# Block 2's short-lived attention buffers in a pool of their own, with residual rows and routing table loaded into its room, and the overflow branch behind the final combine

## The chip, the cores and the metric

The kernel runs on one core of one Trainium2 chip. The metric is the time on the device of one execution, in microseconds (us), as the median of several runs. The engines are named as in the profile: PE multiplies matrices (PEld loads its weights), DVE, ACT and POOL work on rows, SP issues DMA transfers, and ACT and POOL issue some too. The span of a profiled execution runs from its first to its last instruction; the execution's own time is a little longer.

## The reference: two transformer blocks

The input is 512 tokens of 1024 values in fp32. Block 1 is a sparse attention with a state space mixer and a mixture of 16 experts; the change touches it in nothing but a name. Block 2, in outline:

```python
h = rms_norm(x, norm_attn)
q_mla, ckv, k_rope, qkv_dil, gate_pre = split(h @ w_in)
om = mla_branch(q_mla, ckv, k_rope, ...)       # 8 heads, causal softmax attention
od = dilated_branch(qkv_dil, ...)              # 3 groups (dilation 1, 4, 16), merged by their log sums
m  = gate0 * (om @ w_o_mla) + gate1 * (od @ w_o_dil)
x  = x + m @ w_out
hf = rms_norm(x, norm_ffn)
combine = top 2 of the 8 experts of the best of 4 groups, with weights   # T x 32
for e in range(32):
    y += combine[:, e:e+1] * ((silu(hf @ w_gate[e]) * (hf @ w_up[e])) @ w_down[e])
out = x + y
```

## The kernel before: stages, pools and the places that the change touches

The 512 tokens are NT = 4 tiles of 128 rows (P). Products in fp32 are made of three products of split halves: `whi`, `wlo` for weights, `ahi`/`alo`-like names (`hhi`, `mhi`, `mlo`, `odh`, `odl`, `omh`, `oml`) for rows. ACT copies the high half, DVE or POOL subtract it for the low one. A scheduler that follows the program with times of its own sets the order of the instructions on each engine; waits follow from buffers and data. Buffers come from pools, stacked on the left and the right side of the on-chip memory. A pool's room can be taken by the next one only when all that used it are done.

Block 2 runs `block2`, from the main function: projections, MLA attention (`mla_att`), three dilated groups (`dil_att`), whose results go to DRAM (`accd`), and gates. The **merge** follows. `merge_groups` (L1555 on) reads the small tables `nmd`, forms the factors `mcf` (ACT, L1569), and for each tile loads three `da` (SP, L1583), multiplies them by the factors (DVE, L1585) and adds them up in `od` (POOL, L1587). PE turns `od` over (into a bank `tp`, L266), ACT and DVE split it into `odh` and `odl` (L173, L174). `split_mla` does the same for the MLA output `omT` (L1601, L1602). `merge_out` multiplies both by the halves of `wo`, applies the gates (`ga`, `gb`), and splits the sum into `mhi`, `mlo`. Then the product with `wo2` is added to the **residual rows** `xo` (DVE, L1897), four tiles that SP loads from DRAM (`xr`, L1866). The router's weight table `wr` is loaded by ACT (L768, in `moe_open`) and multiplied by the norm's gains `cl` on POOL (L1876). Both live in pool `rt2`, which is opened when block 2's pool `b2` is closed.

The **second mixture** is `moe_experts_rows`, for 32 experts with 64 places each. The weights of each expert are streamed (SP, L823: `raw` and `rawp`, from `in_wgu` and `in_wd`). PE gathers the tokens of four experts by a one-hot matrix (`sel`, L1164), multiplies by gate and up (`gu`, L1179), and by down (`down`, L1208). The weighted result `yy` (ACT for odd, DVE for even experts; L1218, L1220) has two buffers, and POOL scatters it with an adding indirect DMA into `xa` in DRAM (L1221). `xa` holds the rows that the experts' results are added to. The last LAST = 2 experts stay on the chip: `tokens` and `combined` add them with matmuls. SP loads the four tiles of `xa` back (`spare<-xa`, L1227) when all scatters are in.

The **end**: `moe_overflow` reads a count (L1263) and branches around its body when it is zero (L1264); the body handles tokens that found no place in their expert. Every engine has its own copy of the branch. Behind it, the main function combines: 32 matmuls (L1257), two banks `sc` and `pv` in turn, eight adds (L1924), four stores by ACT and SP in turn (L1925).

## Time and profile before

| | us |
|---|---|
| median of 3 runs | 1420.57 |
| lowest and highest of them | 1415.96, 1423.95 |
| the profiled execution, its own time | 1421.81 |
| its span | 1420.0 |

| engine | busy, us | share of the span |
|---|---|---|
| PE | 1313.9 | 93% |
| PEld | 1006.4 | 71% |
| DVE | 776.3 | 55% |
| ACT | 591.3 | 42% |
| POOL | 453.1 | 32% |

Shares over the whole span mix stages with different limits. The merge lies at about 980 to 1108 us of the span, the second mixture's experts at 1118 to 1400, and the end behind them. A row of the timeline gives start, duration, engine, line, operation, and in brackets the idle time just before it with what ended it. A row of waits gives what was waited for, the total in us, the times, and the longest. "L1221" is line 1221 of the kernel before.

### The profile page before, as it was taken

How to read it: one execution, taken by the hardware profiler on the slowest of the kernel's cores; microseconds unless marked ns; L12 is line 12 of the kernel's file. 1: busy time of each engine (PE TensorE's matmuls, PEld its weight loads, DVE VectorE, ACT ScalarE, POOL GpSimd, SP SyncE). 2: the span in 40 equal slices, each digit the busy share in tenths (PEclk: the TensorE clock that was granted, in tenths of full speed). 3: DMA queues.
4: the chain of work that ended last, by engine and by line, in shares of the span. 5: the costliest groups of instructions: out<-in, count | busy, mean ns of one | idle time of the engine just before them, and what ended most of it. 6: DMA issues, size and time to landing. Idle time of an engine off the chain costs nothing. (4 is left out here: it accounts for less than half of the span.)

```text
span 1420.0 us, 21542 instructions
## 1 busy us (share of the span) xinstructions
PE 1313.9 (93%) x8172; PEld 1006.4 (71%) x8188; DVE 776.3 (55%) x1659; ACT 591.3 (42%) x1235; POOL 453.1 (32%) x368
## 2 busy tenths in 40 slices
PE   8898999779999798999999999999989699998976
PEld 8786778756665597977899999887779545444423
DVE  7899964858785756665454353226543623222222
ACT  5466442336665355564654453444323222211211
POOL 3354642422221246531142242215532201111111
PEclk9999999879999899999999999999999899999997
DMA  6122114889997212210111222234249589999993
GB/s 235 60 75 75 45 41 173 303 292 299 315 295 272 96 46 83 90 53 38 60 69 68 76 77 96 69 108 162 89 171 328 191 305 358 365 356 365 368 365 130
DMA packets 68980, 250.77 MB, mean 177 GB/s; under 512 B 12354, under 2 KB 12610, under 8 KB 62720
## 3 DMA queue, kind: packets, MB, share of 16 engines
q1 hardware_dynamic: 56304, 220.90, 43.2%
q0 software_dynamic: 11408, 25.24, 6.6%
q10 hardware_dynamic: 1152, 3.12, 0.6%
q8 instruction: 68, 1.11, 0.3%
q14 instruction: 48, 0.39, 0.1%
HBM read 230.29 MB, written 26.71 MB: 181 GB/s over the span
## 5 line engine op out<-in xcount | busy, mean ns | idle before, releaser
L154 POOL TENSOR_TENSOR wlo<-raw,whi 128x1024 fp32r<-128x1024 f32 (+4 forms) x62 | 149.4, 2412 | 250.3 <-ACT whi L153 250.3
L153 ACT ACTIVATE whi<-raw 128x1024 fp32r<-128x1024 f32 (+4 forms) x172 | 178.3, 1038 | 95.8 <-PE mm L183 41.9
L154 DVE TENSOR_TENSOR wlo<-raw,whi 128x1024 fp32r<-128x1024 f32 (+3 forms) x110 | 142.6, 1296 | 100.7 <-ACT whi L153 100.3
L1221 POOL DMA_INDIRECT xa<-yy,idx x30 | 46.6, 1553 | 223.0 <-DMA xa<-yy,idx 146.1
L183 PE MATMUL mm<-whi,hRl 128*128 128x256 f32 x384 | 109.5, 286 | 0.0
L181 PE MATMUL mm<-whi,hhi 128*128 128x256 f32 (+2 forms) x352 | 103.7, 294 | 5.0 <-ACT qraw L1412 1.9
L1179 PE MATMUL mm<-raw,xe 128*64 128x512 f32 x396 | 101.3, 620 | 4.5 <-ACT xe L1168 4.5
L183 PE MATMUL mm<-whi,hlo 128*128 128x256 f32 (+2 forms) x352 | 102.8, 292 | 0.0
L181 PE MATMUL mm<-whi,hRh 128*128 128x256 f32 x352 | 102.6, 291 | 0.0
L182 PE MATMUL mm<-wlo,hhi 128*128 128x256 f32 (+2 forms) x352 | 102.1, 290 | 0.0
L182 PE MATMUL mm<-wlo,hRh 128*128 128x256 f32 x352 | 99.8, 283 | 0.0
L271 POOL TENSOR_TENSOR hss<-hss,mh 128x4 f32<-128x4 f32 (+1 forms) x64 | 60.0, 939 | 103.8 <-DVE hss L270 92.6
L181 PEld LDWEIGHTS mm<-whi,hhi 128*128 128x128 f32 x352 | 69.4, 197 | 10.7 <-issue 3.8
L1186 DVE TENSOR_TENSOR gul<-gul,mm 64x512 f32<-64x512 f32 x32 | 21.9, 685 | 100.1 <-ACT gul L1185 99.9
L183 PEld LDWEIGHTS mm<-whi,hRl 128*128 128x128 f32 x384 | 74.0, 193 | 0.0
L1164 PEld LDWEIGHTS pv<-sel,xh 128*128 128x128 f32 x256 | 49.6, 194 | 29.9 <-issue 25.8
L182 PEld LDWEIGHTS mm<-wlo,hhi 128*128 128x128 f32 x352 | 69.5, 197 | 1.6 <-issue 1.4
L183 PEld LDWEIGHTS mm<-whi,hlo 128*128 128x128 f32 x352 | 69.5, 197 | 1.4 <-issue 1.1
L1164 PE MATMUL pv<-sel,xh 128*128 128x256 f32 x256 | 67.3, 298 | 2.1 <-issue 2.1
L181 PEld LDWEIGHTS mm<-whi,hRh 128*128 128x128 f32 x352 | 67.2, 191 | 0.2
L182 PEld LDWEIGHTS mm<-wlo,hRh 128*128 128x128 f32 x352 | 67.3, 191 | 0.0
L1179 PEld LDWEIGHTS mm<-raw,xe 128*64 128x64 f32 x396 | 28.2, 141 | 53.2 <-issue 43.4
(533 smaller groups left out, 3685.4 us busy)
## 6 DMA issues: line engine op xcount, KB each, us to landing
raw<-in_wgu SPq DMA_DIRECT2D x163, 512.0 KB, 6.2
raw<-in_wd SPq DMA_DIRECT2D x77, 512.0 KB, 6.3
raw<-in_w2b SPq DMA_DIRECT2D x26, 1024.0 KB, 4.9
rawp<-in_wgu SPq DMA_DIRECT2D x29, 512.0 KB, 5.6
raw<-in_wo SPq DMA_DIRECT2D x12, 1024.0 KB, 4.8
rawp<-in_wd SPq DMA_DIRECT2D x19, 512.0 KB, 5.8
raw<-in_w1b SPq DMA_DIRECT2D x8, 1024.0 KB, 4.9
spare<-xa SPq DMA_DIRECT2D x8, 512.0 KB, 4.9
```

Of the source, the lines that this page charges most:

```text
L153: self.nc.scalar.activation(hi[:, :n], src, AF.Copy)
L154: eng.tensor_tensor(lo[:, :n], src, hi[:, :n].bitcast(F32), op=OP.subtract)
L181: nc.tensor.matmul(ps, lh, rh, start=start and i == 0, stop=False)
L182: nc.tensor.matmul(ps, lh, rl, start=False, stop=False)
L183: nc.tensor.matmul(ps, ll, rh, start=False, stop=stop and i == n - 1)
L271: return self.nc.gpsimd.tensor_tensor(out, out, self.mh[:, :n], op=OP.pow)
L1164: nc.tensor.matmul(pg[:, j * 256:(j + 1) * 256], part[t][:, c], sels[e][:, t].rearrange("p e s -> p (e s)"), start=(i == 0), stop=(i == le ...
L1179: nc.tensor.matmul(pg[j * T:(j + 1) * T], x[:, 2 * c + j, e % 4], w[:, j * 512:(j + 1) * 512], start=(c == 0), stop=(c == 3))
L1186: V.tensor_tensor(lo, lo, pg[o * T:(o + 1) * T], op=OP.add)
L1221: nc.gpsimd.indirect_dma_start(out=xa2, out_offset=bass.IndirectOffsetOnAxis(ap=self.idx[:, 0, e:e + 1], axis=0), in_=y, in_offset=None, b ...
```

## The change

1. Block 2's short-lived tiles (the probabilities `pr` and their turned copies `pe`, the MLA output `omT`, the dilated groups' `ab` and `row`) come from a pool `bs` of their own on the right side ("b2s") and not from `b2`. In block 1 the name stands for the old pool.
2. `block2` takes a function and calls it ahead of `merge_out`. It closes that pool, opens `rt2` in its room, and there issues the loads of the four `xo`, and `moe_open` with the load of `wr`. The pool of the weights, `mw2`, is opened after `b2` is closed, as before.
3. The experts' results get three buffers (NY = 3) of twice the width, of which one half is used, in place of two.
4. The final combine stands in `moe_experts_rows`, ahead of `moe_overflow`. It uses the banks `sc`, `pv`, `mm` and `tp`, and the last tile is stored in two halves, by SP and ACT. In the overflow body, each tile is stored again.

```diff
-        pr = self.b1.tile([P, 512], F32, tag="pr", name="pr", bufs=self.NPR)
+        pr = self.bs.tile([P, 512], F32, tag="pr", name="pr", bufs=self.NPR)
...
-        omT = self.omT = b1.tile([P, 4, S], F32, name="omT")
+        omT = self.omT = self.bs.tile([P, 4, S], F32, name="omT")
...
-            y = me.tile([P, 512], F32, tag="yy", name="yy", bufs=2)
+            y = me.tile([P, D], F32, tag="y", name="yy", bufs=self.NY)[:, :512]
...
+        for t in range(NT):
+            x = self.base[t]
+            for n in range(2):
+                c = slice(n * 512, (n + 1) * 512)
+                o = bank(("sc", "pv", "mm", "tp")[2 * (t % 2) + n])
+                self.combined(o, t, n)
+                V.tensor_tensor(x[:, c], x[:, c], o, op=OP.add)
+                if t == NT - 1:
+                    (nc.sync, nc.scalar)[n].dma_start(self.A["out"][t * P:(t + 1) * P, c], x[:, c])
+            if t < NT - 1:
+                self.store(t, x)
         self.moe_overflow(me)
+
+    def store(self, t, x):
+        (self.nc.sync if t % 2 else self.nc.scalar).dma_start(self.A["out"][t * P:(t + 1) * P, :], x)
...
                 if rows is None:
                     nc.sync.dma_start(self.xa[t * P:(t + 1) * P, :], acc)
+                else:
+                    self.store(t, acc)
...
-    def block2(self):
+    def block2(self, then):
+
...
+        then()
         self.merge_out()
...
         with self.pool("b1") as self.b1:
+            self.bs = self.b1
             self.block1()
...
+        nmw, nme = 19, 1
+        self.LAST = 2
+        self.NX, self.NY, self.FLIGHT = 0, 3, 4
+        self.FIRST = 3
+        xs, xl, short = [], [], ExitStack()
+
+        def experts2():
+
+            short.close()
+            rt = mws.enter_context(right("rt2"))
+            for t in range(NT):
+                xs.append(rt.tile([P, D], F32, tag=f"xo{t}", name=f"xo{t}"))
+                nc.sync.dma_start(xs[t], self.xr[t * P:(t + 1) * P, :])
+            xh = rt.tile([P, NT, D], F32R, name="xh")
+            self.moe_open(32, 64, A["wr2"], self.r("br2"), A["wgu2"], A["wd2"], rt, None, 0, ([xh[:, t] for t in range(NT)], xl))
         with self.pool("b2") as self.b1:
+            self.bs = short.enter_context(right("b2s"))
             self.dmat = self.b1.tile([P, 512], BF, name="dmat")
             dm = self.g("dm")
             nc.scalar.dma_start(dm, A["dm"])
             nc.vector.tensor_copy(self.dmat, dm)
-            self.block2()
-        rt = mws.enter_context(right("rt2"))
-        xs = [rt.tile([P, D], F32, tag=f"xo{t}", name=f"xo{t}") for t in range(NT)]
-        xl = []
-        for t in range(NT):
-            nc.sync.dma_start(xs[t], self.xr[t * P:(t + 1) * P, :])
-        nmw, nme = 19, 1
-        self.LAST = 2
-        self.NX, self.NY, self.FLIGHT = 0, 2, 4
-        self.FIRST = 3
+            self.block2(experts2)
+        rt, xh = self.rt, self.rows[0]
+        self.mw = mws.enter_context(right("mw2"))
+        self.places = [(self.mw, f"raw{i}") for i in range(nmw)]
         xp = ph.enter_context(self.pool("x2"))
-        xh = rt.tile([P, NT, D], F32R, name="xh")
         self.pp = xp
-        self.moe_open(32, 64, A["wr2"], self.r("br2"), A["wgu2"], A["wd2"], rt, mws.enter_context(right("mw2")), nmw,
-                      ([xh[:, t] for t in range(NT)], xl))
...
         self.moe_mid(ph, None, "2", nme)
-        for t in range(NT):
-            x = self.base[t]
-            for n in range(2):
-                c = slice(n * 512, (n + 1) * 512)
-                o = self.bank(("sc", "pv")[n])
-                self.combined(o, t, n)
-                nc.vector.tensor_tensor(x[:, c], x[:, c], o, op=OP.add)
-            (nc.sync if t % 2 else nc.scalar).dma_start(A["out"][t * P:(t + 1) * P, :], x)
         mws.close()
```

What this does to the order of instructions is shown at three places. SP's queue at the merge, first before, then after:

```order
L1583 DMA da<-accd_73 128x512
L146 DMA raw<-in_wo 128x2048
L1583 DMA da<-accd_71 128x512
...
L146 DMA raw<-in_wo 128x2048 x5
L1866 DMA xo_11273<-xr 128x1024
...
L146 DMA raw<-in_wo 128x2048
L823 DMA raw<-in_wgu 128x1024 x12
```

```order
L1599 DMA da<-accd_73 128x512
L1887 DMA xo_10970<-xr 128x1024
...
L146 DMA raw<-in_wo 128x2048
L1599 DMA da<-accd_71 128x512
...
L146 DMA raw<-in_wo 128x2048 x5
L823 DMA raw<-in_wgu 128x1024 x2
L146 DMA raw<-in_wo 128x2048
L823 DMA raw<-in_wgu 128x1024 x10
```

The four loads of `xo` moved from behind the five `wo` loads to behind the first six `da` loads, ahead of the other six; two weight loads of the experts moved ahead of the last `wo` load.

POOL at the merge's start, before and after (`oml` is the low half of the MLA output):

```order
L1602 TENSOR_TENSOR oml<-omT,omh 128x512 x3
L154 TENSOR_TENSOR wlo<-raw,whi 128x1024
L1587 TENSOR_TENSOR od<-od,da 128x512 x5
L154 TENSOR_TENSOR wlo<-raw,whi 128x1024
L1587 TENSOR_TENSOR od<-od,da 128x512 x3
...
L772 MEMSET ml 128x4x8
L774 MEMSET m_11293 128x32
L1876 TENSOR_TENSOR wr<-wr,cl 128x288
```

```order
L1618 TENSOR_TENSOR oml<-omT,omh 128x512 x3
L154 TENSOR_TENSOR wlo<-raw,whi 128x1024
L772 MEMSET ml 128x4x8
L774 MEMSET m_10984 128x32
L1902 TENSOR_TENSOR wr<-wr,cl 128x288
L1603 TENSOR_TENSOR od<-od,da 128x512 x4
L154 TENSOR_TENSOR wlo<-raw,whi 128x1024
L1603 TENSOR_TENSOR od<-od,da 128x512 x4
```

The two memsets and the product of `wr` moved from behind the merge to ahead of the first sum `od`. On ACT the load of `wr` stands right behind `mcf` now. DVE at the same place, before and after:

```order
L1585 TENSOR_TENSOR da<-da,mcf 128x512 x2
L1585 TENSOR_TENSOR od<-da,mcf 128x512
L154 TENSOR_TENSOR wlo<-raw,whi 128x1024
...
L1585 TENSOR_TENSOR da<-da,mcf 128x512 x2
L174 TENSOR_TENSOR odl<-tp,odh 128x4x128 x2
```

```order
L154 TENSOR_TENSOR wlo<-raw,whi 128x1024
L174 TENSOR_TENSOR odl<-tp,odh 128x4x128
L1601 TENSOR_TENSOR od<-da,mcf 128x512
L1601 TENSOR_TENSOR da<-da,mcf 128x512
L174 TENSOR_TENSOR odl<-tp,odh 128x4x128
L1601 TENSOR_TENSOR da<-da,mcf 128x512
```

The first two `odl` moved from behind the last multiplication to between them.

PE at the program's end, before and after (`cnti` is the count of the overflow):

```order
L1257 MATMUL pv<-spare 128x512 x8
L1263 TENSOR_LOAD cnti
L1264 COMPARE_AND_BRANCH
...
L1264 UNCONDITIONAL_BRANCH
L1257 MATMUL sc<-spare 128x512 x8
L1257 MATMUL pv<-spare 128x512 x8
L1257 MATMUL sc<-spare 128x512 x8
L2087 UNCONDITIONAL_BRANCH
```

```order
L1271 MATMUL sc<-spare 128x512 x4
L1271 MATMUL pv<-spare 128x512 x3
L1271 MATMUL mm<-spare 128x512 x3
L1271 MATMUL tp<-spare 128x512 x3
L1277 TENSOR_LOAD cnti
L1278 COMPARE_AND_BRANCH
...
L1278 UNCONDITIONAL_BRANCH x2
```

All 32 matmuls of the combine stand ahead of the load of the count and the branch. SP's queue at the same place has the four loads of the base rows, a store of 128x1024, the store of 128x512, and then its branch; before, the branch stood behind the four loads and the two stores behind the branch.

## Rows read from the trace of the kernel before

**Rows 1.** Windows: stretch, length, busy (x) of PE, PEld, DVE, ACT, POOL; clock; DMA; GB/s.

```profile
1040.00:1060.00 20.00, 16.25 (x100) 14.26 (x99) 8.95 (x10) 4.00 (x6) 7.44 (x7) 1.00 0.43 147
1160.00:1380.00 220.00, 203.06 (x1050) 95.70 (x1048) 59.16 (x104) 42.33 (x78) 40.28 (x26) 0.98 1.01 363
1400.00:1408.00 8.00, 2.55 (x10) 1.32 (x8) 2.79 (x4) 0.74 (x2) 0.00 (x0) 0.80 0.71 268
1408.00:1420.00 12.00, 7.26 (x24) 5.82 (x24) 3.95 (x6) 0.00 (x0) 0.00 (x0) 0.64 0.44 177
```

**Rows 2.** Waits of SP's queue, 1100 to 1420 us.

```profile
SPq L823 <- DMA raw<-in_wgu: 100.0, 77, 5.4
...
SPq L1264 <- SPq L1264: 5.9, 2, 5.4
```

**Rows 3.** Waits of the engines, 1160 to 1400 us.

```profile
POOL xa L1221 <- DMA xa<-yy,idx: 146.1, 22, 7.9
...
ACT yy L1218 <- DMA xa<-yy,idx: 63.1, 11, 13.8
```

**Rows 4.** Timeline of POOL, scatters of the experts' results.

```profile
1326.96 1.54 POOL L1221 DMA_INDIRECT xa<-yy,idx  x1 [8.61 <-DVE yy L1220]
...
1385.56 1.55 POOL L1221 DMA_INDIRECT xa<-yy,idx  x1 [6.19 <-DMA xa<-yy,idx]
1390.00 1.54 POOL L1221 DMA_INDIRECT xa<-yy,idx  x1 [2.89 <-DVE yy L1220]
1394.89 1.54 POOL L1221 DMA_INDIRECT xa<-yy,idx  x1 [3.35 <-DMA xa<-yy,idx]
```

**Rows 5.** Timeline of all engines at the merge's end.

```profile
1053.42 1.95 SPq L1866 DMA_DIRECT2D xo<-xr  x4
...
1057.58 0.76 DVE L1897 SCALAR_TENSOR_TENSOR xo<-mm,xo 128x256 f32<-128x256 f32 x2 [4.23 <-DMA xo<-xr]
1057.68 0.67 POOL L1876 TENSOR_TENSOR wr<-wr,cl 128x288 f32<-128x288 f32 x1 [4.08 <-DMA wr<-in_wr]
...
1058.06 0.38 PE L181 MATMUL mm<-whi,mhi 128*128 128x256 f32 x1 [2.96 <-DVE xo L1897]
```

**Rows 6.** DMA issues, 960 to 1060 us: KB each, median us to landing.

```profile
wr<-in_wr ACTq DMA_DIRECT2D x1, 144.0 KB, 4.2
```

**Rows 7.** Timeline of all engines at the merge's start.

```profile
980.50 0.28 ACT L1569 ACTIVATE mcf<-mcf 128x96 f32<-128x96 f32 x1 [2.79 <-DVE mcf L1568]
...
983.89 3.37 POOL L1587 TENSOR_TENSOR od<-od,da 128x512 f32<-128x512 f32 x2 [3.90 <-DVE da L1585]
```

**Rows 8.** Timeline of PE at the merge's start.

```profile
991.30 0.66 PE L266 MATMUL tp<-cf,od 128*128 128x128 f32 x4 [1.07 <-POOL od L1587]
...
1000.46 0.63 PE L266 MATMUL tp<-cf,od 128*128 128x128 f32 x4 [2.33 <-DVE odl L174]
```

**Rows 9.** Timeline of SP's queue, the last weight load and the base rows.

```profile
1379.19 0.33 SPq L823 DMA_DIRECT2D rawp<-in_wd  x1
1399.03 1.75 SPq L1227 DMA_DIRECT2D spare<-xa  x4
```

**Rows 10.** Timeline of all engines from 1395 us: PE's combine around the branch.

```profile
1400.97 2.43 PE L1257 MATMUL pv<-spare 64*128 64x512 f32 x8 [0.79 <-ACT spare L1213]
...
1408.15 2.47 PE L1257 MATMUL sc<-spare 64*128 64x512 f32 x5 [4.75 <-PEq L1264]
```

**Rows 11.** Line L1264, the branch: ns min, median, max; first and last start.

```profile
L1264 PEldq COMPARE_BRANCH  x2: 3368/3844/4320, 291.5 to 1403.5; - x2
```

**Rows 12.** Tile `spare`, 1395 to 1420 us: ns min, median, max; starts.

```profile
L1924 DVE TENSOR_TENSOR spare<-spare,sc x4: 680/688/689, 1410.2 to 1415.4; 128x512 f32<-128x512 f32 x4
...
L1925 SPq DMA_DIRECT2D out_dram<-spare x2: 338/338/338, 1412.6 to 1416.2; - x2
...
DMA to landing us min/median/max: 2.6/3.1/6.5
```

**Rows 13.** Line L2087, the program's end: SP's part.

```profile
L2087 SPq EVENT_SEMAPHORE  x14: 17/28/28, 1416.6 to 1420.0; - x14
```

More of the change, by code (lines that the diff above doesn't have):

```diff
@@ L1481, in tr @@
                 last = h % 2 and kb == NT - 1
-                pt = self.g("pt")[:, kb * P:] if last else b1.tile([P, S - kb * P], F32, tag=f"p{h % 2}{kb}", name="pe")
+                pt = self.g("pt")[:, kb * P:] if last else self.bs.tile([P, S - kb * P], F32, tag=f"p{h % 2}{kb}", name="pe")
                 pv[h % 2, kb] = pt
@@ L1692, in dil_att @@
         N = 256 if g == 0 else P
-        ab = b1.tile([P, 2048], BF, tag="ab", name="ab")[:, :8 * N].rearrange("p (h n) -> p h n", h=8)
+        ab = self.bs.tile([P, 2048], BF, tag="ab", name="ab")[:, :8 * N].rearrange("p (h n) -> p h n", h=8)
         dm = self.dmat[:, 0:256] if g == 0 else self.dmat[:, 128 + g * 128:256 + g * 128]
@@ L1705, in score @@
                 if q == 0:
-                    sh["row"] = b1.tile([P, 528], F32, tag="row", name="row", bufs=2)
+                    sh["row"] = self.bs.tile([P, 528], F32, tag="row", name="row", bufs=2)
                 row = sh["row"]
@@ L1718, in score @@
                     V.tensor_reduce(row[:, 512 + h0:512 + h0 + 2 * nh - 1:2], sv[par], axis=AX.X, op=OP.max, negate=True)
-                    p = b1.tile([P, 512], F32, tag="pr", name="pr", bufs=self.NPR)
+                    p = self.bs.tile([P, 512], F32, tag="pr", name="pr", bufs=self.NPR)
                     pr.append(p)
@@ L1889, in rows @@
             nc.vector.scalar_tensor_tensor(row, x, s_[:, 3:4], gf, op0=OP.mult, op1=OP.mult)
-            a = nc.scalar.activation(xh[:, t], row, AF.Copy)
+            a = nc.scalar.activation(xh[t], row, AF.Copy)
             xl.append(rt.tile([P, D], F32R, tag=f"xo{t}", name="xl"))
-            b = nc.gpsimd.tensor_tensor(xl[t], row, xh[:, t].bitcast(F32), op=OP.subtract)
+            b = nc.gpsimd.tensor_tensor(xl[t], row, xh[t].bitcast(F32), op=OP.subtract)
             self.order = [a, b]
```

## The prediction

> **What bounds the kernel now.** I read the stretches first, then the waits of each queue, then single rows of the two places that the change touches: the merge of block 2 and the program's last 20 us.
>
> The stretch from 1160 to 1380 us is the second mixture of experts. Its DMA share is 1.01 at 363 GB/s [rows 1], and SP, which issues the weights, spends 100.0 us there and around it only on waits for earlier weights of the gate and up matrices to land [rows 2]. A second thing is as tight. POOL scatters the result of one expert after the other into the sum in DRAM, and each scatter must have landed before the next one starts: POOL waits 146.1 us for that [rows 3]. From 1326.96 to 1385.56 there are seven steps, 8.37 us each [rows 4]. PE is busy for 203.06 of 220 us, but nobody who ends last waits for it.
>
> The merge, just ahead, is PE's: its few gaps there are real time, because PE works without a pause afterwards and everything behind moves with it. The last gap of the merge is the 2.96 us at 1058.06. PE waits for DVE to empty a bank, and DVE had waited 4.23 us for the residual rows `xo`, which SP asked for only at 1053.42 [rows 5]. At the merge's start PE waits 1.07 us for POOL's sum `od` and 2.33 us for DVE's low half `odl` [rows 8].
>
> The end is a chain of its own. The last weights are asked for at 1379.19, the base rows at 1399.03, when the last scatter is in [rows 9]. PE starts the combine at 1400.97, stops after 8 of its 32 matmuls, and goes on at 1408.15. Its sequencer is in the branch around the overflow code, which took 4.32 us at this place [rows 10, 11]. In 1400 to 1408 PE works 2.55 us [rows 1].
>
> **The change part by part.** All sums are made against the profiled execution: span 1420.0 us, whole time 1421.81 us. The median of the runs shown is 1420.57 us, 1.24 us less, and I forecast that median.
>
> A, the residual rows. Their four loads go from behind the five `wo` loads to the merge's start, some 70 us earlier (POOL's first `od` at 983.89 stands there [rows 7]). DVE then finds them there, and the wait of 2.96 us goes [rows 5]. Next late would be the low half of the merged rows for the same tile, but PE has passed that already at this place. I take -3.0. It can't be more, since the gap is no longer; it is 0 if another input of that eviction is late. The 2 MB now stand ahead of six `da` loads and one `wo` load on SP's queue, and this is costed in B.
>
> B, the merge's start. The routing table `wr` is loaded by ACT after `mcf` (ready at 980.50 + 0.28 = 980.8 [rows 7]) and lands 4.2 us after its issue [rows 6], so at 985.0. POOL now multiplies it, 0.67 us [rows 5], before its first `od`, which would start at 985.7 in place of 983.89 [rows 7]: a wait added, 1.8 us. Queued behind it on POOL are all eight `od` sums and the `wlo` split between them, and PE's transposes wait for them. The gap of 1.07 us, which already ends on POOL, grows by up to 1.8. Against this, DVE takes the first two `odl` between the multiplications instead of after all of them, and PE's transposes of the third and fourth tile stand among matmuls that need no new input. I count the gap of 2.33 us as gone. What is next late is `od` of the later tiles, with a slack I can't read. Net: 1.8 - 2.33 = -0.5, and since part of the `wr` wait falls into slack of the first transpose, I take **-0.8**. Lower end: both gaps close and the delay is hidden, -(1.07 + 2.33) = -3.4. Upper end: no gap closes and the delay shows at two tiles, 2 x 1.8 = +3.6; contention of the `xo` loads with `da` would act in the same way and at the same place.
>
> C, the third result buffer. ACT waits 63.1 us in all, over 11 times, to write an expert's result, because both buffers are still being scattered [rows 3]. A third buffer removes most of these waits. But the scatters follow each other whether or not results are ready early, so the stage doesn't become shorter by 63 us. A gain is to be had only where a scatter waited for a result: at 1326.96, where POOL's idle time of 8.61 us ends on DVE, and at 1390.00 [rows 4]. The first is about 1 us longer than the others of its kind, the second at most a few tenths. I take -1.3, with 0 and -1.6 as bounds. The other effect is that PE gets ahead by one expert, so one scatter step of 8.4 us: it would start the combine near 1392.6 instead of 1400.97. This is what makes D possible.
>
> D, the tail. Before, the chain is: PE's branch, 24 matmuls, adds, stores; the last store starts on SP at 1416.2 [rows 12], and the end code runs from 1416.6 to 1420.0, 3.4 us [rows 13]. After, all 32 matmuls come ahead of the branch and write to four kinds of banks in turn in place of two, so the bound is the base rows. SP's four loads start at 1399.03 and take 1.75 us to issue, the last starting near 1400.4; the slowest landing is 6.5 us, so the last tile is in at 1406.9 [rows 9, 12]. An add takes 0.69 us [rows 12]. The first half of the last tile is done at 1407.6; SP has issued its store by 1407.9. The second half is done at 1408.3, and ACT issues it. Now SP's branch stands behind its last store. Before, SP took it at 1400.8, while the base rows were loading, and the 5.4 us that it waited there [rows 2] cost nothing. That cover is gone: 1407.9 + 5.4 = 1413.3, and of the end code's 3.4 us, which includes the wait for the last landing, I leave 2.0, so the end is at 1415.3, **-4.7**. PE's branch, up to 4.32 us, runs beside it from about 1408. Lower end: SP's branch hides and only the end code follows the second store, 1408.65 + 3.4 = 1412.0, so -8.0. Upper end: the base rows land 0.8 us later beside the stores of the first tiles and all 3.4 us follow the branch, 1417.5, so -2.5.
>
> [...]
>
> Costed at nothing: the pool of its own changes addresses only, the overflow body isn't entered in this run, and its additional stores don't execute.
>
> Sum: -3.0 - 0.8 - 1.3 - 4.7 = **-9.8 us**. The profiled execution would be 1412.0, the median 1410.8.
>
> **The rivals.** First, the small gain. POOL's wait for `wr` shows twice or `xo` delays `da`, so B is +1.0 to +3.6; C is near 0; SP's branch and the full end code follow the store, D = -2.5. With A at -3.0 that is -5 to -2, so 1415.6 to 1418.6. This is also the case in which the change doesn't do what it says: the scatters set the stage, and a buffer more gives nothing. For it: the scatter waits are 146.1 us. Against it: A is a wait of one named load, and the tail's branch on PE is plainly idle time.
>
> Second, the large gain: both gaps at the merge's start close (-3.4), SP's branch is hidden or short (-8.0), A -3.0, C -1.3: -15.7, so 1404.9. [...] Against it: SP showed the wait under load, and POOL has a new wait at the merge's start.
>
> [...]
>
> **How the numbers follow.** The forecast has a chance of 0.45 and a range of its own of 1407 to 1413.5. The small gain has 0.27, the large one 0.20, the slower case 0.08, of which half lies within 0.5%. About 0.5% (7.1 us) is what a measurement of this kernel can tell from no change, so faster means under 1413.5 and slower over 1427.7. Faster: 0.45 + 0.20 = 0.65. Same: 0.27 + 0.04 = 0.31. Slower: 0.04. The range from 1403 to 1419 leaves out the slower case and the outer part of the two gains.
>
> **What would show it.** In the profile of the changed kernel: no wait of DVE or PE on `xo` at the merge's end (A). POOL's wait for `wr` ahead of the first `od`, with PE's waits at its transposes from `od` summing to less than 3.4 us (B). ACT's waits for scatters nearly gone, the scatter spacing still 8.4 us (C). PE's combine without a branch in it, starting clearly before 1400; the adds ending on the base loads; SP's branch as the last wait, about 5 us (D). The prediction is wrong if the scatter spacing changes, if PE rather than the base rows ends the tail, or if the merge's start loses more than its end gains.

## The result, and the profile after

The changed kernel takes 1406.45 us, median of 4 runs (1405.88 to 1408.74), beside 1422.26 us for the kernel before in the same comparison. The ratio is 0.9897, 95% interval 0.9874 to 0.992; it comes from all runs and is not the quotient of the two medians, which is 0.9889. A second comparison (f1) gave 0.9898 (0.9873 to 0.9922). By these ratios, which the text uses for gains, it is faster by about 14.5 us; the forecast was 1410.8 us, 9.8 us less than before, with a range from 1403 to 1419.

The profiled execution took 1408.74 us with a span of 1407.0 us, 13.0 us less than the 1420.0 of before. I compare stages from one fixed point, the start of ACT's row for `mcf` (980.50 before [rows 7], 975.75 after), because the 4.75 us ahead of it belong to code whose order of instructions is the same in both kernels (more on this below).

The merge's start, timeline of POOL, then of PE, then of ACT's queue, in the changed kernel:

```profile
975.25 0.12 POOL L774 MEMSET m<- 128x32 f32 x1
982.44 0.68 POOL L1902 TENSOR_TENSOR wr<-wr,cl 128x288 f32<-128x288 f32 x1 [7.07 <-DMA wr<-in_wr]
983.08 5.19 POOL L1603 TENSOR_TENSOR od<-od,da 128x512 f32<-128x512 f32 x4
```

```profile
985.74 1.00 PE L266 MATMUL tp<-cf,od 128*128 128x128 f32 x4 [2.57 <-POOL od L1603]
```

```profile
975.89 0.34 ACTq L768 DMA_DIRECT2D wr<-in_wr  x1
```

POOL stands still for 7.07 us for the table, and its first `od` starts 7.33 us after `mcf`, against 3.39 us before [rows 7]: 3.9 us late. PE waits 2.57 us for it at its first transpose. Before, PE didn't wait at this transpose (timeline of before, PE):

```profile
987.78 0.60 PE L266 MATMUL tp<-cf,od 128*128 128x128 f32 x4
```

The gaps of 1.07 and 2.33 us further on [rows 8] are gone. Two new ones stand behind them, 0.86 and 0.29 us for DVE's `gb` and `ga`. And right behind PE's stop the granted clock is 0.50, the lower of the two levels that this trace's records hold (0.50 and 1.00), where before it stayed at 1.00 (windows, in the form of [rows 1]):

```profile
986.00:989.00 3.00, 3.00 (x10) 2.52 (x9) 1.59 (x3) 0.60 (x1) 2.92 (x3) 0.50 0.71 208
```

The merge's end, timeline of DVE and of SP's queue:

```profile
1048.35 2.21 DVE L174 TENSOR_TENSOR mlo<-ga,mhi 128x512 fp32r<-128x512 f32 x1 [2.13 <-ACT mhi L173]
1051.04 0.42 DVE L1923 SCALAR_TENSOR_TENSOR xo<-mm,xo 128x256 f32<-128x256 f32 x1 [0.48 <-PE mm L183]
```

```profile
972.31 1.80 SPq L1887 DMA_DIRECT2D xo<-xr  x4
```

The residual rows are asked for 79 us ahead of their use. DVE waits for PE there, and no longer for a DMA [rows 5].

The mixture, waits from 1160 to 1400 us, and the last three scatters on POOL's timeline:

```profile
POOL xa L1221 <- DMA xa<-yy,idx: 136.5, 21, 7.8
...
ACT yy L1218 <- DMA xa<-yy,idx: 23.1, 4, 9.5
```

```profile
1375.73 1.55 POOL L1221 DMA_INDIRECT xa<-yy,idx  x1 [5.02 <-DMA xa<-yy,idx]
1380.30 1.54 POOL L1221 DMA_INDIRECT xa<-yy,idx  x1 [3.02 <-DMA xa<-yy,idx]
1384.90 1.54 POOL L1221 DMA_INDIRECT xa<-yy,idx  x1 [3.06 <-ACT spare L1213]
```

ACT's waits for scatters fell from 63.1 [rows 3] to 23.1 us. The scatters still wait for each other. The last row names ACT, but its step from the scatter before, 4.60 us, is that of the row above, 4.57 us, so nothing shows that it waited for more than the scatter before.

The end, timeline of all engines, then the windows (stretch, length, busy time of PE, PEld, DVE, ACT, POOL, clock, DMA share, GB/s), then SP's waits from 1385 us:

```profile
1384.88 0.48 PE L1271 MATMUL sc<-spare 64*128 64x512 f32 x1 [0.81 <-ACT spare L1213]
...
1388.71 2.01 SPq L1227 DMA_DIRECT2D spare<-xa  x4
1392.05 0.69 DVE L1253 TENSOR_TENSOR spare<-spare,sc 128x512 f32<-128x512 f32 x1 [6.46 <-DMA spare<-xa]
...
1399.08 0.34 SPq L1255 DMA_DIRECT2D out_dram<-spare  x1
1399.68 0.34 ACTq L1255 DMA_DIRECT2D out_dram<-spare  x1
```

```profile
1385.00:1391.00 6.00, 3.89 (x32) 3.29 (x32) 0.59 (x1) 0.00 (x0) 1.44 (x1) 1.00 0.40 85
1391.00:1403.00 12.00, 0.00 (x0) 0.00 (x0) 5.14 (x8) 0.00 (x0) 0.00 (x0) 0.55 0.90 323
1403.00:1407.00 4.00, 0.00 (x0) 0.00 (x0) 0.00 (x0) 0.00 (x0) 0.00 (x0) 0.50 0.01 4
```

```profile
SPq L1278 <- SPq L1278: 3.8, 1, 3.8
```

PE starts the combine at 1384.88, together with the last scatter, and has started all 32 matmuls, 3.89 us of work at the full clock (granted 1.00), before the base rows are asked for at 1388.71. Then PE has nothing to do. From 1391 to 1403 the DMA engines are busy for 0.90 of the time, with 2 MB of base rows in and 2 MB of results out. Before, they had a share of 0.71 and 0.44 in the last 20 us [rows 1].

All traces of this study, in us from the start of `mcf` (in the first column: the start of `mcf` itself). "transpose" is PE's first transpose of `od`, "pairs" is the last `gb` of the merge, "gather" the first matmul with `sel`, "sc28" and "last" the third last and the last scatter of a kernel with 30 scatters, "combine" PE's first matmul of the combine, "base" the first base load. The experiments are described below:

| trace | mcf | transpose | pairs | gather | sc28 | last | combine | base | end |
|---|---|---|---|---|---|---|---|---|---|
| before | 980.50 | 7.28 | 67.83 | 140.93 | 405.06 | 414.38 | 420.46 | 418.53 | 439.54 |
| before, again (g1) | 979.34 | 7.25 | 67.81 | 143.08 | 407.44 | 419.13 | 424.25 | 423.14 | 445.31 |
| changed | 975.75 | 9.98 | 69.78 | 138.49 | 399.97 | 409.14 | 409.12 | 412.96 | 431.21 |
| changed, again (f1) | 977.77 | 10.62 | 70.38 | 139.85 | 400.16 | 409.81 | 409.62 | 413.59 | 431.74 |
| e1 two buffers | 975.60 | 10.09 | 69.85 | 139.46 | 402.92 | 416.19 | 423.24 | 420.00 | 437.56 |
| e2 branch ahead | 976.80 | 10.24 | 69.99 | 138.43 | 400.20 | 409.39 | 409.72 | 413.66 | 431.28 |
| e3 (see there) | 978.71 | 9.99 | 69.29 | 137.36 | 399.75 | 409.10 | 410.18 | 412.93 | 431.15 |
| e4 stores by ACT | 976.84 | 9.99 | 69.76 | 140.47 | 401.34 | 410.56 | 410.47 | 414.31 | 431.82 |
| f2 three buffers only | 980.85 | 7.28 | 67.81 | 141.77 | 403.29 | 412.55 | 413.22 | 416.82 | 435.81 |
| f3 branch last only | 975.55 | 7.28 | 67.81 | 141.08 | 402.74 | 413.06 | 419.88 | 417.30 | 435.03 |
| f4 merge only | 977.04 | 9.99 | 69.30 | 137.68 | 398.00 | 407.78 | 414.27 | 411.54 | 433.33 |
| g2 three kept | 975.95 | 11.38 | 71.12 | 139.59 | - | 405.31 | 401.73 | 409.41 | 427.73 |
| g3 four kept | 978.34 | 10.30 | 70.05 | 138.67 | - | 401.81 | 399.22 | 405.72 | 432.66 |
| h1 (see there) | 974.22 | 10.05 | 69.36 | 138.07 | - | 403.39 | 398.07 | 407.61 | 424.74 |

One trace of a kernel differs from the next by some us (the two of before by 2.2 us at the first gather, 2.4 at the third last scatter, 4.8 at the last and 5.8 at the end), so the text below goes by means over all traces that share a part.

### The profile page after: what moved, and what is told of

Its sections match the earlier page's. It is cut to its first block, busy times and chain, and to the rows that moved or that the text cites. A ratio compares the mean times of both kernels' runs of the same rounds, so it can differ in the third digit from the quotient of the medians.

```text
span 1407.0 us, 21509 instructions
## 1 busy us (share of the span) xinstructions
PE 1303.7 (93%) x8172; PEld 998.5 (71%) x8188; DVE 774.0 (55%) x1659; ACT 591.6 (42%) x1235; POOL 452.1 (32%) x368
## 4 chain that ended last, share of the span: by engine, by line
PE 76%; DVE 13%; DMA 5%; ACT 2%; issue 2%; POOL 1%; SPq 0%; DVEq 0%; ACTq 0%; POOLq 0%
PE mm L181 13%; PE mm L183 13%; PE mm L182 13%; PE mm L1179 8%; PE tp L266 5%; PE pv L1164 5%; PE sc L1208 3%; DMA xa<-yy,idx 2%; PE pv L1759 2%; PE mm L1051 2%; DVE work L409 1%; DVE m L408 1%; PE sc L1733 1%; PE sc L1489 1%; DVE pr L707 1%
## 5 line engine op out<-in xcount | busy, mean ns | idle before, releaser
L1186 DVE TENSOR_TENSOR gul<-gul,mm 64x512 f32<-64x512 f32 x32 | 21.9, 686 | 92.4 <-ACT gul L1185 92.4
L1164 PE MATMUL pv<-sel,xl 128*128 128x256 f32 x256 | 65.6, 292 | 0.0
```

Source lines behind the costliest of these rows:

```text
L1164: nc.tensor.matmul(pg[:, j * 256:(j + 1) * 256], part[t][:, c], sels[e][:, t].rearrange("p e s -> p (e s)"), start=(i == 0), stop=(i == le ...
```

## The experiments

**e1, two buffers.** The third buffer is taken away, nothing else moves.

```diff
-        self.NX, self.NY, self.FLIGHT = 0, 3, 4
+        self.NX, self.NY, self.FLIGHT = 0, 2, 4
```

> The changed kernel with two result buffers in the second mixture in place of three, nothing else moved. Theory (the third buffer pays): the changed kernel gained 3.4 us between its first and its last scatter, and its combine began at 1384.9, ahead of the base rows. With two buffers the last scatter is 3 us later, and PE's combine starts about 6 us behind the last scatter, as before, so it ends the tail: 1409 to 1413 us against 1406.5. Rival (the scatters follow each other at their own pace, and a late PE is hidden by the loads of the base rows): within 1.5 us of 1406.5, with ACT waiting some 60 us for scatters again.

Measured: 1412.98 us, ratio to before 0.9939 (0.992 to 0.9958). From `mcf` to the end it took 437.56 us, 6 us more than the changed kernel. Waits from 1160 to 1400 us, the timeline of the last scatters, and PE and SP at the end:

```profile
POOL xa L1221 <- DMA xa<-yy,idx: 153.9, 23, 8.5
...
ACT yy L1218 <- DMA xa<-yy,idx: 66.0, 10, 13.9
```

```profile
1323.98 1.54 POOL L1221 DMA_INDIRECT xa<-yy,idx  x1 [9.95 <-DVE yy L1220]
...
1373.41 0.69 ACT L1218 ACTIVATE yy<-sc,gs 128x512 f32<-128x512 f32 x1 [8.26 <-DMA xa<-yy,idx]
1376.39 0.69 PE L266 MATMUL tp<-cf,gul 128*128 128x128 f32 x2 [5.32 <-DVE gul L1188]
...
1378.52 1.55 POOL L1221 DMA_INDIRECT xa<-yy,idx  x1 [2.93 <-DMA xa<-yy,idx]
1387.24 1.54 POOL L1221 DMA_INDIRECT xa<-yy,idx  x1 [7.16 <-DVE yy L1220]
1391.79 1.54 POOL L1221 DMA_INDIRECT xa<-yy,idx  x1 [3.01 <-ACT gul L1187]
```

```profile
1398.84 0.48 PE L1271 MATMUL sc<-spare 64*128 64x512 f32 x1 [0.81 <-ACT spare L1213]
```

```profile
1395.61 1.75 SPq L1227 DMA_DIRECT2D spare<-xa  x4
```

ACT waits 66.0 us again. The row at 1387.24 shows what it costs: the second last scatter stands 7.16 us for DVE's result. ACT had waited 8.26 us for a scatter to free its buffer, and PE, whose next transpose needs rows that ACT and DVE prepare, 5.32 us behind that. The chain is fast there (the scatter after 1378.52 could have come 4.5 us later, as the one after 1387.24 did), so a late result costs time at once. The combine starts 7.05 us behind the last scatter instead of with it. The theory held by the trace, where the third buffer is worth about 6 us. The run times say less: in this comparison e3, which is the changed kernel (see there), took 1407.61 us, 0.9921, so the difference is 5.4 us by the medians and 2.6 by the ratios, whose intervals overlap.

**e2, branch ahead again.** The combine is moved behind the branch, as before the change, with its two banks and whole stores; three buffers stay.

```diff
-        for t in range(NT):
-            x = self.base[t]
...
-            if t < NT - 1:
-                self.store(t, x)
         self.moe_overflow(me)
...
         self.moe_mid(ph, None, "2", nme)
+        for t in range(NT):
+            x = self.base[t]
+            for n in range(2):
+                c = slice(n * 512, (n + 1) * 512)
+                o = self.bank(("sc", "pv")[n])
+                self.combined(o, t, n)
...
```

> The changed kernel with the overflow branch ahead of the final combine again, two banks and four whole stores as before the change. [...] The last store is followed by the end code alone: 1403 to 1405 us, 2 to 3 us less than the changed kernel's 1406.5. Rival (the new place of the combine is what gained in the tail): 1409 us, since the tail from the base loads to the end took 20.97 us before and 18.29 us after the change.

Measured: 1410.9 us, 0.994 (0.9921 to 0.9959). Timeline of all engines at the end:

```profile
1386.52 2.45 PE L1260 MATMUL pv<-spare 64*128 64x512 f32 x8 [0.79 <-ACT spare L1213]
1390.46 1.75 SPq L1227 DMA_DIRECT2D spare<-xa  x4
1392.24 2.90 PE L1260 MATMUL sc<-spare 64*128 64x512 f32 x6 [3.27 <-PEq L1267]
1393.91 0.69 DVE L1937 TENSOR_TENSOR spare<-spare,pv 128x512 f32<-128x512 f32 x1 [6.65 <-DMA spare<-xa]
```

PE is out of its branch at 1392.24, 1.67 us ahead of DVE's first add, which waits for the first base row until 1393.91: in this trace the loads cover the branch. But nothing is gained: 431.28 us from `mcf` to the end, against 431.21 and 431.74 for the changed kernel. The 2 to 3 us that were expected did not come. The run times lean to the rival: 3.3 us more than e3, the changed kernel in the same comparison, by the medians and 2.7 by the ratios, with intervals that overlap. In the trace the place of the branch makes no difference to the end, and the two parts of it that do differ are told under D below.

**e3, routing table late.** The load of `wr` is written behind `block2`, so that POOL needn't wait for it at the merge's start.

```diff
-        self.nc.scalar.dma_start(self.wgt.rearrange("p k w -> p (k w)"), wr)
+        if rows is None:
+            self.nc.scalar.dma_start(self.wgt.rearrange("p k w -> p (k w)"), wr)
...
+        nc.scalar.dma_start(self.wgt.rearrange("p k w -> p (k w)"), A["wr2"])
         nc.gpsimd.tensor_tensor(self.wgt, self.wgt, self.l("nf")[:, :, None].to_broadcast([P, KT, 36]), op=OP.mult)
```

> The changed kernel with the load and the product of the routing table behind the merge again; the residual rows stay early. Theory (POOL's wait for the table is what the merge's start lost): PE's gap of 2.57 us ahead of its first transpose goes, a gap of about 1 us at the second comes back: 1404.5 to 1405.5 us against 1406.5. Rival (the multiplications on DVE and the da loads, late behind the 2 MB of residual rows, hold the transposes): the gap stays, and the time is within 0.7 us of 1406.5.

Measured: 1407.61 us, 0.9921 (0.9893 to 0.9949). POOL's timeline:

```profile
985.40 0.69 POOL L1904 TENSOR_TENSOR wr<-wr,cl 128x288 f32<-128x288 f32 x1 [7.07 <-DMA wr<-in_wr]
986.05 5.19 POOL L1604 TENSOR_TENSOR od<-od,da 128x512 f32<-128x512 f32 x4
```

The experiment failed: the product stands where it stood and waits the same 7.07 us, because the scheduler put load and product into the same place on every engine. It tells nothing of the theory and is a third trace of the changed kernel. That POOL's wait for the table holds up the merge's start is read from the rows, not tested by undoing it.

**e4, all stores by ACT.** SP then has nothing behind its base loads but the branch.

```diff
-                    (nc.sync, nc.scalar)[n].dma_start(self.A["out"][t * P:(t + 1) * P, c], x[:, c])
+                    nc.scalar.dma_start(self.A["out"][t * P:(t + 1) * P, c], x[:, c])
...
-        (self.nc.sync if t % 2 else self.nc.scalar).dma_start(self.A["out"][t * P:(t + 1) * P, :], x)
+        self.nc.scalar.dma_start(self.A["out"][t * P:(t + 1) * P, :], x)
```

> The changed kernel with all stores of the result issued by ACT, so that SP stands in its branch while the base rows are still loading. Theory (SP's branch, 3.83 us from its compare to the next semaphore, ends the program): SP is through by about 1395, the last landing decides, and the time is 2 to 3 us less, 1403.5 to 1404.5 us against 1406.5. Rival (ACT's queue with five stores, its count load of 0.70 us and its own branch take the place): 1406 to 1407 us.

Measured: 1410.56 us, 0.9931 (0.9906 to 0.9956); 431.82 us from `mcf` to the end. Windows of the end:

```profile
1394.00:1405.00 11.00, 0.00 (x0) 0.00 (x0) 5.14 (x8) 0.00 (x0) 0.00 (x0) 0.52 0.89 336
1405.00:1408.70 3.70, 0.00 (x0) 0.00 (x0) 0.00 (x0) 0.00 (x0) 0.00 (x0) 0.50 0.02 6
```

SP came to its branch at 1393.64, 15 us ahead of the end, and the end didn't move. The theory fell, and its rival's 1406 to 1407 us didn't come either (e3 in the same comparison: 1407.61). SP's waits from 1385 us show what the row of 3.8 us in the changed kernel was:

```profile
SPq L1278 <- SPq L1278: 12.4, 1, 12.4
```

In the changed kernel's trace, SP's first instruction behind the branch waits for the semaphore of the last store (number 100, of ACT's store at 1399.68). That instruction starts at 1406.08 here and at 1403.30 in the changed kernel, 0.5 and 0.4 us after the last packet of the result has landed (1405.61 and 1402.90, from the traces' DMA records). So SP's branch is not what ends the program; the 4 MB are, at a DMA share of 0.89 until 1405, with 3.0 us from the last landing to the end.

**f1, the changed kernel again,** beside the three parts alone; f2 to f4 start from the kernel before.

> The changed kernel as it is, beside its single parts on the same chip. Theory (the first comparison holds): a ratio of 0.988 to 0.992 to the kernel before, so 1405 to 1409 us, and the same times from the factors mcf to the end as its first profile, 431.2 us, within 1 us. Rival (part of the first comparison was a lucky start, since 4.8 us of the profiled 13 lay ahead of the merge, where the kernels hardly differ): a ratio of 0.993 to 0.995.

Measured: 1408.16 us beside 1421.19 us, 0.9898 (0.9873 to 0.9922), and 431.74 us from `mcf`. The theory held.

**f2, three buffers only.**

```diff
-            y = me.tile([P, 512], F32, tag="yy", name="yy", bufs=2)
+            y = me.tile([P, D], F32, tag="y", name="yy", bufs=self.NY)[:, :512]
...
-        self.NX, self.NY, self.FLIGHT = 0, 2, 4
+        self.NX, self.NY, self.FLIGHT = 0, 3, 4
```

> The kernel before with nothing but the third result buffer. Theory (the third buffer brings PE ahead of the scatters, and then PE's branch is covered by the loads of the base rows): 6 to 8 us less than before, 1412 to 1414 us, with the combine starting no later than the last scatter. Rival (the forecast's term, the scatters set the pace): 1 to 2 us less, 1418 to 1419 us.

Measured: 1414.07 us, 0.9943 (0.9921 to 0.9964): 8 us less than before. Timeline, last scatter and combine:

```profile
1393.41 1.54 POOL L1221 DMA_INDIRECT xa<-yy,idx  x1 [3.21 <-ACT spare L1213]
1394.08 2.46 PE L1257 MATMUL pv<-spare 64*128 64x512 f32 x8 [0.79 <-ACT spare L1213]
```

The combine starts 0.67 us behind the last scatter (the theory had said no later than it), not 6.08 us as before [rows 4, 10]. The theory's time held, the forecast's 1 to 2 us didn't.

**f3, branch last only.** The new combine stands ahead of the branch; two buffers, merge as before. The edit is that part of the diff.

> The kernel before with nothing but the new end: combine ahead of the branch, four kinds of banks, last tile in halves. Theory (it repairs the late PE's stop in the branch, and nothing more): from the base loads to the end 17.5 to 18.3 us in place of 21.0, so 3 us less, 1416 to 1417.5 us. Rival (the forecast's D): 4.7 us less, 1415 us. Second rival (a late combine at the low clock): no gain, 1419 to 1421 us.

Measured: 1415.96 us, 0.9961 (0.9941 to 0.9981), 5.5 us less. From the base loads to the end it takes 17.7 us in place of 21.0 and 22.2, as the theory said; the forecast's 4.7 us fits the time as well. PE's 32 matmuls, though late, ran in 3.64 us from their first to their last start (419.88 to 423.52 after `mcf`), so the low clock of the second rival didn't come.

**f4, merge only.** The own pool, `then()`, and the early loads; two buffers, branch ahead.

> The kernel before with nothing but the own pool and the early residual rows and routing table; two result buffers, branch ahead of the combine. Theory (the merge's end gains 3 us and its start loses 2, and the mixture begins about 2 us earlier): 1417 to 1418.5 us, 1.5 to 2.5 us less. Rival (the mixture is paced by weights and scatters and gives it back): 1419 to 1420.5 us.

Measured: 1416.37 us, 0.9964 (0.9946 to 0.9982), 5.1 us less, more than either number expected; from `mcf` to the first gather its trace gains 4.0 us on the mean of the four with the old merge (A and B below). PE's combine is cut in two again (timeline):

```profile
1391.31 2.41 PE L1260 MATMUL pv<-spare 64*128 64x512 f32 x8 [0.79 <-ACT spare L1213]
1398.48 2.47 PE L1260 MATMUL sc<-spare 64*128 64x512 f32 x5 [4.76 <-PEq L1267]
```

The three parts alone give 8.1 + 5.5 + 5.1 = 18.7 us, the whole change 14.5. The difference of 4.2 us is within the intervals of these ratios, so the run times alone don't show that the parts overlap. The traces do: the third buffer and the moved branch cure the same stop of PE, as the time from the last scatter to the end shows:

| last scatter to end, us | branch ahead of the combine | branch last |
|---|---|---|
| two buffers | 25.2, 26.2, 25.6 (before, g1, f4) | 22.0, 21.4 (f3, e1) |
| three buffers | 23.3, 21.9 (f2, e2) | 22.1, 21.9, 22.1, 21.3 (changed, f1, e3, e4) |

Either one brings it to 21.4 to 23.3 us, one or two traces each; both together bring no more.

**g1, the kernel before again.**

> The kernel before, unchanged, for a second trace. Theory (the 4.8 us by which the two first traces differ ahead of the merge are chance, drops of the granted clock): mcf starts anywhere from 975 to 981 us, and from mcf to the end it takes 439.5 us as in the first trace, within 2 us. Rival (the kernel before is longer in the mixture too, and its first trace was a short one there): 441 to 446 us from mcf to the end.

One execution, 1426.42 us, 445.31 us from `mcf` to the end: the rival's number, but not its place. Of the 5.8 us by which this trace is longer, 2.2 are there at the first gather already, 0.2 come up to the third last scatter, 2.4 with the last two scatters and 1.0 behind them. The first trace's own time, 1421.81 us, is close to the medians of before (1419.75 to 1422.74 in five comparisons), while 1426.42 us lies near the top of its runs. Taken together, before needs 442.4 us from `mcf` (two traces), the changed kernel 431.4 (three, with e3): 11.1 us of the 14.5.

**g2, keep three experts on the chip.** Since the end is the last scatter and 4 MB behind it, one scatter less should end it earlier.

```diff
-        self.LAST = 2
+        self.LAST = 3
```

> The changed kernel with the last three experts kept on the chip in place of two (48 matmuls in the combine, one scatter less). Theory (the end is: last scatter, then 4 MB of base rows and stores through the DMA engines, 18.2 us): the base rows are asked for one scatter earlier, 4.6 us, and the combine's 16 more matmuls at 0.12 us fit ahead of them: about 4 us less than the changed kernel, a ratio of 0.986 to 0.988 to the kernel before. Rival (PE's combine then ends the tail): within 1.5 us of the changed kernel, 0.989 to 0.991.

Measured: 1404.57 us, 0.9881 (0.9851 to 0.9911). From `mcf`: last scatter 405.31, base loads 409.41, end 427.73. SP's timeline, the last weight load and the base loads:

```profile
1373.02 0.33 SPq L823 DMA_DIRECT2D rawp<-in_wd  x1
1385.36 1.75 SPq L1227 DMA_DIRECT2D spare<-xa  x4
```

The trace shows the 4 us that the theory asked for: 18.3 us from the base loads to the end, as in the changed kernel (18.25), with the loads 3.9 us earlier. The ratio lies between the two numbers, and its interval holds both.

**g3, keep four,** with the base loads written behind the last weight load. (LAST = 4, and the loop over the base loads at the last expert, under an order that was to keep it behind the weights.)

> The changed kernel with the last four experts kept on the chip (64 matmuls in the combine, two scatters less, three of the four base loads ahead of the last weight load). Theory (last scatter and 4 MB): the base rows are asked for 9 us earlier, but PE is done with its 64 matmuls only 4 us after it is now, so 5 to 7 us less than the changed kernel, a ratio of 0.984 to 0.987. Rival (the last weights wait behind the base rows, and PE's combine ends the tail): 0.988 to 0.992.

Measured: 1406.26 us, 0.99 (0.9864 to 0.9936), 432.66 us from `mcf` in the trace, whose run of 1412.85 us is near the longest of its six. SP's timeline and PE's:

```profile
1384.06 1.28 SPq L1220 DMA_DIRECT2D spare<-xa  x3
1385.39 0.42 SPq L823 DMA_DIRECT2D rawp<-in_wd  x1
```

```profile
1392.37 1.97 PE L1208 MATMUL sc<-rawp,hT 128*64 128x512 f32 x4 [2.13 <-DMA rawp<-in_wd]
```

The rival's case came: the last weight load stood behind three base loads that waited for the last scatter, and PE waited for it until 1392.37.

**h1, three on the chip, table late.**

> The changed kernel with the last three experts kept on the chip and the routing table's load and product behind the merge. Theory (the two gains lie in different stages; keeping three took 3.7 us off the end, the late table about 1 us off the merge's start, of which the mixture may give back any part): 426.5 to 428 us from the factors mcf to the end, against 431.2 and 431.7 in the two traces of the changed kernel, and a ratio of 0.985 to 0.989 to the kernel before. Rival (what the end gained was chance of one trace): 430.5 to 432 us from mcf to the end, a ratio of 0.990 to 0.993.

Measured: 1404.8 us beside 1422.74 us, 0.9881 (0.9857 to 0.9904); 424.74 us from `mcf` to the end, below both numbers. As in e3, the table's product stayed where it was (POOL waited 7.14 us for it), so this is g2 a second time. Its two traces, 427.73 and 424.74 us, lie below all three of the changed kernel, by 5.1 us in the mean. Both versions with three kept beat the kernel before. Against the changed kernel their two ratios (0.9881 twice) are lower than its 0.9897 and 0.9898, but the intervals overlap.

## Why the prediction was right, point by point

**What bounds the kernel** was read rightly: the mixture kept its pace (DMA share 1.01, scatters one behind the other), and only what lies ahead of it, at its last scatters and behind it moved.

**A, the residual rows: right.** Forecast -3.0. PE's gap of 2.96 us is gone; matched PE instructions around it shift by 3.2 us between before and f1, f4 and e4. From the last pair to the first gather the kernels gain more, 5.0 us in the means (73.9 in four traces with the old merge, 68.9 in ten with the new). Of the other 1.8 us, 1.1 are mostly the clock: the forecast priced the wait by the first trace of before, in which PE goes on at full clock behind it. In g1 the granted clock is 0.50 behind the same stop (windows of g1), and in f3 it is 0.51 for 3 us:

```profile
1057.00:1063.00 6.00, 5.93 (x28) 5.93 (x29) 0.75 (x3) 0.72 (x2) 0.37 (x1) 0.50 1.01 391
```

Matched PE instructions come 2.9 us later there in g1, 1.2 in f3 and 0.3 in f2 than in the first trace, 1.1 in the mean of the four. In the ten traces with the new merge the granted clock is 1.00 around this place. The last 0.7 us were not taken apart.

**B, the merge's start: wrong in sign, inside its bounds.** Forecast -0.8, bounds -3.4 and +3.6; measured +2.1 us at the last pair (67.8 in four traces, 69.9 in the mean of the ten with the new merge). The step that failed is the landing of the table. I took the 4.2 us of [rows 6]; that load was issued together with the residual rows [rows 5], on DMA engines that had been idle (a share of 0.00 from 1053 to 1054). Timeline of before, ACT's queue:

```profile
1053.43 0.36 ACTq L768 DMA_DIRECT2D wr<-in_wr  x1
```

Now 2 MB of residual rows, issued 2.2 to 3.6 us earlier, and more loads are under way in front of it (a DMA share of 1.02 from 972 to 982), and from its issue at 975.89 to POOL's start at 982.44 it took 6.55 us. So POOL started 3.9 us late, not 1.8. The second half of the step, that the later gaps close, came true, but PE's waits in the merge's start add up to 3.7 us, as before, since two new ones opened. Part of the rest is the clock, which the sum didn't have: in seven of the ten traces it falls to 0.50 behind PE's stop for `od`, and these have their last pair at 70.1 us in the mean, the three without it at 69.3.

**C, the third buffer: right in kind, too small.** Forecast -1.3, at most -1.6. From the first gather to the last scatter it takes 273.7 us in five traces with two buffers and 270.7 in six with three: -3.0. Up to the third last scatter the difference is 1.4 us (262.8 and 261.4), which is the size of the term I had. Its place can be seen too: the step to the 21st scatter, the late one of [rows 4], takes 9.0 to 11.5 us in the five traces with two buffers (10.2 in the mean) and 7.7 to 9.0 in the six with three (8.3). The totals overlap, though: single traces with two buffers take from 270.1 to 276.7 us, with three from 270.0 to 271.7. The other 1.6 us are the last two scatters (10.9 and 9.3 us from the third last to the last). I had allowed tenths of a microsecond there from one row [rows 4]; in the second trace of before a scatter waits 5.37 us for DVE at this place, and in e1 one waits 7.16. Where weights no longer load the DMA engines (a share of 0.19 from 1375 to 1385 in the changed kernel), a scatter followed the last one after 4.6 us, and a late PE showed.

PE ahead by one expert: forecast 8.4 us, measured 6.0 (combine 6.3 us behind the last scatter with two buffers, 0.3 with three).

**D, the end: size near, reason wrong.** Forecast -4.7, measured -3.6 (25.6 to 22.0 us from the last scatter to the end, in the table above). It is not SP's branch that holds the end. In the changed kernel SP goes on 3.8 us after its compare, but in all nine traces with the branch last it does so 0.4 to 0.6 us after the last packet of the result has landed, whether the branch was reached 4 or 12 us earlier (e4). What the branch alone costs SP there is not shown: the landing covers it. With the branch ahead SP goes on 5.3 to 5.5 us after its compare in five traces, 2.6 to 3.9 us after DVE has used the first base row; that is the wait that I had read.

What takes the branch's place is the transfer of 4 MB at 0.9 of the DMA engines. From the first base load to the last landing it takes 14.2 to 14.5 us in three traces of the changed kernel, against 19.7 to 20.9 in before, g1 and f4: 6.0 us less. My sum had SP's branch end 14.3 us behind the base loads, which is the right number for another reason, so luck. Behind the landing the term was too small: I left 2.0 us for the end code, and it took 3.6 to 4.1, where with the branch ahead it takes 1.3 to 1.4. So moving the branch to the end costs some 2.5 us behind the landing (1.8 in f3, where only the end was changed), and of the 6.0 us 3.5 are left. The base rows landed later than in the sum as well, while stores of the first tiles ran beside them: last add 10.9 us behind the base loads, against my 9.3. And the gain isn't the moved branch's alone: with three buffers the end stands at the same place with the branch ahead (e2), where the last store, a whole tile, lands 16.2 us behind the base loads, 1.9 us later, and the end follows 2.4 us sooner. Whether halves of the last tile with the branch ahead would gain both was not tried.

**Sum.** A and the rest of the merge's end -5.0, B +2.1, C -3.0, D -3.6: -9.5 us, beside the forecast's -9.8. That they agree is luck: the errors of the terms cancelled. The measured 14.5 us (11.4 to 17.9 by the interval) are more, and 1406.45 us lies just below the forecast's own range of 1407 to 1413.5. The traces account for most of the rest: the two of before and the three of the changed kernel differ by 13.6 us in span, 11.1 behind `mcf` and 2.5 ahead of it, where I had forecast nothing. The four traces with the old pools reach `mcf` at 979.1 us in the mean (975.6 to 980.9), the ten with the new ones at 976.7 (974.2 to 978.7). The order of instructions there is the same. What goes with it is the clock: PE spends 44 to 65 us at a granted clock of 0.50 ahead of `mcf`, 58.0 in the mean with the old pools and 51.9 with the new, and `mcf` comes the later the more of it there is (a correlation of 0.90 over the 14 traces). One place stands out: windows of 540 to 560 us have a granted clock of 0.88, 0.89 and 0.88 in three of four traces with the old pools, and of 1.00 in nine of the ten with the new ones (0.91 in e3). Whether the other addresses of the buffers do that, or chance, stays open.

**The rivals.** The small gain fell with f2, f3 and f4: every part alone is faster. It was half right on B. The large gain's time, 1404.9 us, lies nearest to the result, but not for its reasons: the merge's start wasn't hidden, and SP's branch was, but behind the landing of the last store, which its sum didn't have. The slower case has a chance of 0.08 in the forecast, and no run shows it: each part alone was faster than before, and e1 and f3, whose combine starts late (423.24 and 419.88 us after `mcf`), still do the 32 matmuls in under 4 us, in one go. Of the signs named ahead, two came out differently: ACT's waits for scatters are not nearly gone (22.7 to 34.6 us in the three traces of the changed kernel), and SP's last wait, 3.8 us, is for a landing.

## What to carry to other kernels

When results go through a slow serial step, a third buffer did little for the pace of that step here (1.4 us up to the third last scatter), but it decided how far behind the producer was when the step ended (6.3 us with two buffers, 0.3 with three), and the tail paid for that. Before pricing a wait at the end of a program, ask what else runs under it and which semaphore the instruction behind it waits for: here 4 MB of transfers ran, and the wait ended 0.4 to 0.6 us after they had landed. Two cures for the same stop of PE could not both be counted: the last scatter to the end took 21.4 to 23.3 us with either and 21.3 to 22.1 with both. A load that is moved early can be a load in front of others: the table's took 6.55 us behind 2 MB and more, not the 4.2 us of before, so price the ones behind it with it under way, not by their landing on engines that were idle when they were issued.

## What the runs showed of the hardware

A scatter of one expert's rows was followed by the next after 8.4 us while the weights streamed (DMA share 1.01), and after 4.6 us when they were through (1375.73, 1380.30, 1384.90; DMA share 0.19 from 1375 to 1385). The load of 144 KB took 4.2 us when it was issued together with 2 MB on another queue, on idle DMA engines, and 6.55 us behind loads that kept them at a share of 1.02. SP's first instruction behind its branch started 0.4 to 0.6 us after the last packet of the result in nine traces, and 5.3 to 5.5 us after its compare in the five where base rows were still loading. Behind a stop of 2.6 to 4.0 us PE's granted clock was at 0.50 or 0.51 in nine of 14 traces (behind the wait for `od` in seven, behind that for `xo` in two). Two traces of one kernel differed by up to 5.8 us from the same point to the end.
